# A hybrid scan and convolution layer on one core: the latent convolution's result kept in 8 KB rows and gathered by the loads, four scan output buffers, and one transfer per kernel block

## The chip, the cores and the metric

The kernel runs on one core of a Trainium2 chip. The metric is the device time of one execution in microseconds (us). The engines are TensorE (PE; PEld is its weight load), VectorE (DVE), ScalarE (ACT), GpSimd (POOL) and SyncE (SP). SPq and ACTq are the instruction queues of SP and ACT, from which transfers (DMAs) are issued in program order; sixteen DMA engines carry them.

## The reference

One layer of a diffusion backbone is computed for 256 context tokens and for 2048 latent tokens, which lie on a grid of 32 rows of 64. Each token's normalised and modulated vector is projected; one part goes through a bidirectional scan (SSD), another through a gated depthwise convolution, and both are joined in an output projection.

```python
h = rms_norm(x, g_pre) * (1 + scale) + shift
u = h @ w_in
z, xbc, dt_raw, ga, gb, gsil = jnp.split(u, [I_Z, I_XBC, I_DT, I_GA, I_GB], axis=-1)
y_ssd, h_fin = ssd_branch(z, xbc, dt_raw, ...)
# conformer_branch: convolution of 31 taps over the grid's rows, for each channel and column
h = ga * jax.nn.sigmoid(gb)
h = depthwise_conv(h, conv_w, conv_b)
h = layer_norm(h, ln_g, ln_b)
y_conf = jax.nn.silu(h) * jax.nn.silu(gsil)
out = jnp.concatenate([y_ssd, y_conf], axis=-1) @ w_out
return x + gate * rms_norm(out, g_post), h_fin
```

There are 1024 channels in the convolution, 1024 in the scan (16 heads of 64, state 128, chunks of 128 tokens). All is float32.

## The kernel before

The 2304 tokens are 18 tiles of 128: tiles 0 and 1 are context, 2 to 17 latent. Matmuls keep float32 accuracy by splitting each operand into a high and a low part and multiplying three pairs (`hh,wh`, `hl,wh`, `hh,wl`; lines L433 to L435).

The program has two halves (tiles 0 to 9, then 10 to 17). In each half `xbc_unit` projects the scan's inputs, `gab_unit` the convolution's (result `GL[j]`, by blocks `j` of 128 channels), `silu_unit` the gates. The weights' split parts are stored in the first half and loaded again in the second (`wh<-whd` L390, `wl<-wld` L391, three buffers each).

Beside the projections of the second half run two side streams. One is the scan, `pass_a(i)`, tile by tile: `xT` and `bc` are loaded (L705, L707), decay rows `lb` come by ACTq (L718), are masked on POOL (L730), exponentiated on ACT (L738) and combined on DVE (L742); `skip` (L810) begins the output `yg` of each of two groups, `close` (L815, L817) finishes it and stores it to `YP` (L818). The other is the latent convolution, `lat_conv(j)`: for 128 channels the grid rows `x` (`cx`, L671) and the banded kernel matrices `kd` (L670) are loaded one block ahead; ACT copies `kd` to `kt` (L679); PE does 256 small matmuls `cp` (L690); DVE adds the bias into `vt` (`cvv`, L694), in which a partition holds one of four groups of 32 channels and one grid row, with 32 channels x 64 columns behind it; four stores (L699) write it to `CV`, laid out as channels x tokens.

Then comes the out-projection, from tile 17 down. For each tile `conf_load` reads the 1024 channels of 128 tokens from `CV` (tile `cn`, two buffers, L1183), `conf_sum`, `conf_mean` and so on normalise it, and PE multiplies. The calls in the steady loop are written in program order and kept there for DVE, ACT and PE (those instructions carry the line L81 of the helper); elsewhere, and for the transfers, a list scheduler that works on estimated times sets each engine's order, within which an engine takes its instructions one after the other. A buffer with n copies can be written again only when the readers of the copy n uses before are done.

Of the kernel before, what the change touches and what calls it, by code (L numbers as in the profile page):

```python
# [8 lines left out]
F32 = mybir.dt.float32  # L9
# [8 lines left out]
P = 128  # L18
D = 1024
KT = D // P  # L20
NH = 16
HD = 64
NT = 18
NCTX = 2
# [60 lines left out]
def backbone_kernel(ctx, tc, xa, xt_in, cols, rows, wconv, conf_b, gp_row, bg_row, state0, w_mod, w_dt, w_in, w_out,  # L85
# [3 lines left out]
    V, S, T, DMA = (InOrder(tc, e) for e in (nc.vector, nc.scalar, nc.tensor, nc.sync))  # L89
# [5 lines left out]
    def bank(tag, name):  # L95
        return psp.tile([P, 512], F32, tag=tag, name=name, bufs=3 if tag == "mm" else 5)

    def dram(name, shape):
        return drp.tile(shape, F32, tag=name, name=name)
# [3 lines left out]
    ZS = [dram(f"zs{h}", [D, HT[h] * P]) for h in range(2)]  # L103
    GL = [dram(f"gl{j}", [P, NT * P]) for j in range(KT)]
    GS = [dram(f"gs{h}", [D, HT[h] * P]) for h in range(2)]
    CV = dram("cv", [D, NT * P])
    YP = [dram(f"yp{i}", [P, D]) for i in range(NT)]
    ST = [dram(f"st{i}", [P, D]) for i in range(NT)]
    LT = [dram(f"lt{h}", [HT[h] * 32, P]) for h in range(2)]
# [10 lines left out]
    def place(i):  # L120

        return (0, i) if i < HT[0] else (1, i - HT[0])
# [14 lines left out]
    cv = const.tile([P, NCOL], F32, name="cv")  # L137
# [51 lines left out]
    pa = ph_a.enter_context(tc.tile_pool(name="pa", bufs=1))  # L189
# [450 lines left out]
    def ctx_conv(j, tile):  # L640
        g = tile(f"cg{j}")
        G.memset(g[:, 0:15], 0.0)
        G.memset(g[:, 271:286], 0.0)
        DMA.dma_start(g[:, 15:271], GL[j][:, 0:256])
        yield
        acc = g[:, 512:768]
        w0 = C_CONFW + j * CW
        V.here("tensor_scalar", acc, g[:, 0:256], cv[:, w0:w0 + 1], cfb2[:, j:j + 1], MUL, ADD)
        for t in range(1, CW):
            V.here("scalar_tensor_tensor", acc, g[:, t:t + 256], cv[:, w0 + t:w0 + t + 1], acc, MUL, ADD)  # L650
            if t % 3 == 0:
                yield
        o = g[:, 768:1024]
        S.mul(o, acc, 0.5)
        DMA.dma_start(CV[j * P:(j + 1) * P, 0:256], o)
        yield


# [4 lines left out]
    def lat_load(j, lp):  # L663
        kd = lp.tile([P, 32, 32], F32, tag="kd", name=f"kd{j}", bufs=2)
        x = lp.tile([P, 32, 64], F32, tag="cx", name=f"cx{j}", bufs=2)
        lat_in[j] = kd, x
        for a in range(4):
            rs = slice(a * 32, (a + 1) * 32)
            src = bass.AP(tensor=wconv.tensor, offset=(j * 4 + a) * 64 * 32, ap=[[32, 32], [1, 1024]])
            DMA.dma_start(kd[rs].rearrange("p r g -> p (r g)"), src)  # L670
            DMA.dma_start(x[rs], GL[j][:, 256:].rearrange("(g a) (r w) -> a r g w", a=4, w=64)[a])  # L671

    def lat_conv(j, lp, cbb, more):
        if j not in lat_in:
            lat_load(j, lp)
        kd, x = lat_in.pop(j)
        yield
        kt = lp.tile([P, 32, 32], F32, tag="kt", name=f"kt{j}", bufs=1)
        S.copy(kt[:, :, ::-1].rearrange("p g r -> p r g"), kd)  # L679
        if more(j + 1):  # L680
            lat_load(j + 1, lp)
        yield
        vt = lp.tile([P, 32, 64], F32, tag="cvv", name=f"cvv{j}", bufs=1)
        for h in range(2):
            ps = {a: bank("ss", f"cp{j}_{a}") for a in (2 * h, 2 * h + 1)}
            for q in range(8):
                for u in range(4):
                    for a in ps:
                        rs = slice(a * 32, (a + 1) * 32)
                        T.matmul(ps[a][u * 32:(u + 1) * 32, q * 64:(q + 1) * 64], kt[rs, u * 8 + q, :], x[rs, u * 8 + q, :],  # L690
                                 start=True, stop=True)
            yield
            for a in ps:
                V.scalar_tensor_tensor(vt[:, a::4, :], ps[a].rearrange("p (c w) -> p c w", w=64), 0.5,  # L694
                                       cbb[:, j, a::4].unsqueeze(2).to_broadcast([P, 8, 64]), MUL, ADD)
            yield
        for u in range(4):
            c0 = j * P + u * 32
            DMA.dma_start(CV[c0:c0 + 32, 256:].rearrange("c (r w) -> r c w", w=64), vt[u * 32:(u + 1) * 32])  # L699


    def pass_a(i):
        half, il = place(i)
# [102 lines left out]
        yg = {}  # L806

        def skip(g):
            yg[g] = pa.tile([P, 4, P], F32, tag="yg", name=f"yg{i}{g}", bufs=2)
            V.tensor_tensor(yg[g], xT[:, 4 * g:4 * g + 4, :],  # L810
                            cv[:, C_D + 4 * g:C_D + 4 * g + 4].unsqueeze(2).to_broadcast([P, 4, P]), MUL)

# [35 lines left out]
        decay(0, 1)  # L848
        mask(1, 0)
        skip(0)  # L850
        load_lb(1, 1)
        yield
        weigh(0, 1)
        mix(0, 1)
        decay(1, 0)
        mask(1, 1)
        skip(1)
        yield
        diag(0, 0)
# [131 lines left out]
    V.tensor_tensor(wd4[:, :, 1, :], wdr, wd4[:, :, 0, :].bitcast(F32), SUB)  # L991
    xbc_phase(0, first, hb, [hprep(2, hb), hprep(0, hb)], tails, dt_post(0))
    extra = chain([gate_rows()] + [ctx_conv(j, big) for j in range(4)])
    interleave(post(0, 6), merge(scan(range(9)), 68, extra, 9 + 4 * 13), 90 * 8)
    last = [silu_unit(0, GS0, GS, j, hb, (2, 1, 0)) for j in (6, 7)]
# [19 lines left out]
    lp = ph_l.enter_context(tc.tile_pool(name="lp", bufs=1, side="right"))  # L1015
# [4 lines left out]
    blocks = post(1, 5)  # L1020
    cg = lambda name: lp.tile([P, D], F32, tag="cg", name=name, bufs=2)
    lat = lambda j: lat_conv(j, lp, cbb, gl_done.__contains__)
    extra = chain(f for j in range(4) for f in (lat(2 * j), ctx_conv(j + 4, cg), lat(2 * j + 1)))
    sc_ = scan(range(9, NT))
    run(take(blocks, 24))
# [112 lines left out]
    def norms(i, yz, nq):  # L1138

        pm = bank("ss", f"pm{i}")  # L1140
        src = [(c, e, t[1]) for c, e, t in ((0, 4.0 * EPS, yz), (1, EPS, nq)) if t]
        for c, e, t in src:
            T.matmul(pm[:, c:c + 1], t, ones[:, 0:1], start=True, stop=True)
        rs = []
        for c, e, t in src:
            ms = p1.tile([P, 1], F32, tag=f"ms{c}", name=f"yms{i}{c}", bufs=2)
            V.tensor_scalar(ms, pm[:, c:c + 1], 1.0 / D, e, MUL, ADD)
            rs.append((c, rstd_of(p1, ms, f"yr{i}{c}")))
        return rs
# [30 lines left out]

    def conf_load(i):
        n = p2.tile([P, 8, P], F32, tag="cn", name=f"cn{i}", bufs=2)
        DMA.dma_start(n, CV[:, i * P:(i + 1) * P].rearrange("(c p) t -> p c t", p=P))  # L1183
        return n

    def conf_sum(i, n):
        v = p2.tile([P, 8, P], F32, tag="v", name=f"v{i}", bufs=2)
        return v, sum8(v[:, 0, :], v[:, 0:4, :], n)
# [16 lines left out]
    def gs_load(i):  # L1205
        gs = p2.tile([P, 8, P], F32, tag="gs", name=f"gsl{i}", bufs=1)
        DMA.dma_start(gs, chan_slice(GS, i))
        return gs
# [57 lines left out]
    i = order[0]  # L1266
# [21 lines left out]
    for b in range(2):  # L1288
        for m, u in enumerate(last):
            run(take(u, 8))  # L1290
            if b == 0 and m == 1:
                rs = norms(i, yz, None)
# [3 lines left out]
            if b == 0 and m == 2:  # L1296
                ssd_scale(i, yz[0], spread(i, rs))
                yh = hl(p0, "y", 2, i, yz[0])
                lo(yh)
                yz = y_sum(i1)  # L1300
                for g in range(2):
                    state_decay(i1, g)
                ph_b[1].close()
                p2 = ph_1.enter_context(tc.tile_pool(name="p2", bufs=1))
                nn = [conf_load(i), conf_load(i1)]
                vv = [conf_sum(j, n) for j, n in zip((i, i1), nn)]
                for (v, t), j, n in zip(vv, (i, i1), nn):
                    conf_centre(n, conf_mean(j, t))
                    conf_square(v, n)
                nq = conf_sqsum(i, vv[0][0])  # L1310
            if b == 1 and m == 0:
                rs = norms(i, None, nq)
                nq = conf_sqsum(i1, vv[1][0])
            if b == 1 and m == 1:
                n, v = nn[0], vv[0][0]
# [3 lines left out]
            if b == 1 and m == 2:  # L1319
                gs0, v0, n = gs_load(i), v, nn[1]  # L1320
# [6 lines left out]
    for k in range(9, 13):  # L1327
        wo_load(k, wo4)
    n2 = conf_load(order[2])

    def out_seg(i, y, p, k0, k1):
# [6 lines left out]
    i, nxt, nx2 = order[:3]  # L1338
    banks(i)
    out_part(pso[i], yh, 0, 1)  # L1340
    rs = norms(nxt, yz, nq)
# [21 lines left out]
    v2, t = conf_sum(nx2, n2)  # L1363
# [18 lines left out]
    yz = y_sum(nx2)  # L1382
    ssd_load(order[3])
    n, n2 = n2, conf_load(order[3])
    yh = yhn

    for a, i in enumerate(order[1:], 1):
        last = a + 1 == NT
        e = {1: 4, 2: 2}.get(a, 0)
# [5 lines left out]
        rs = None if last else norms(nxt, yz, nq)  # L1395
# [6 lines left out]
        if nx2 is not None:  # L1402
            st_load(nx2)
            v2, t = conf_sum(nx2, n2)
# [37 lines left out]
        if a + 3 < NT:  # L1442
            ssd_load(order[a + 3])
            n, n2 = n2, conf_load(order[a + 3])
        else:
            n = n2
# [72 lines left out]
```

## Time and profile before

| what | value |
|---|---|
| median of three runs | 1862.05 us (1860.89 to 1865.44) |
| the profiled execution, its time / its span | 1862.69 / 1860.9 us |
| busy share of the span: PE, DVE, ACT, POOL | 97%, 65%, 47%, 9% |
| mean granted clock of PE | 0.983 |
| DMA packets, moved | 304253, 375.22 MB |
| of them under 512 B | 84198 |

The span is what lies between the first and the last instruction of the profile. In a row of the timeline the columns are start, duration, engine, line, operation, output and inputs, count, and in brackets the engine's idle time just before with what ended it. A line like L81 can be a helper's. "issue" means that the profile shows nothing that was waited for.

### The profile page before, as it was taken

What the parts mean: (1) busy time and instruction counts of PE and PEld (TensorE: products, weight loads), DVE (VectorE), ACT (ScalarE), POOL (GpSimd) and SP (SyncE); (2) the same over time, 40 slices, a digit from 0 to 9 for tenths busy, and PEclk for the clock granted to TensorE, in tenths of its full rate; (3) what the DMA queues carried; (4) which work ended last, traced back from release to release, by engine and by line L of the source; (5) the groups of instructions that cost most, each with busy time, mean ns of one, the idle gap of its engine ahead of it and who ended that gap; (6) DMA issues with size and microseconds to landing.
All of it is one profiled execution on the core that took longest, in us unless ns stands there. A gap on an engine that the chain in (4) does not pass through costs nothing.

```text
span 1860.9 us, 29891 instructions
## 1 busy us (share of the span) xinstructions
PE 1797.5 (97%) x11167; PEld 1482.9 (80%) x11167; DVE 1212.7 (65%) x1846; ACT 867.4 (47%) x1958; POOL 167.5 (9%) x281
## 2 busy tenths in 40 slices
PE   5899999999999999999999889899999999999998
PEld 3688887888888888888877667677887888888886
DVE  4488867565666762587457475868347887777763
ACT  4646424444465441834235445553245545454441
POOL 0002001111111000100001011110000111111110
PEclk9899999999999999999999899899999999999999
DMA  9556565574776664446598799685877666566632
GB/s 319 201 202 224 198 222 196 168 237 153 239 271 232 202 214 162 163 152 210 175 223 239 163 255 227 220 226 193 278 237 247 184 184 170 173 171 170 187 102 79
DMA packets 304253, 375.22 MB, mean 202 GB/s; under 512 B 84198, under 2 KB 203622, under 8 KB 304108
## 3 DMA queue, kind: packets, MB, share of 16 engines
q1 hardware_dynamic: 283372, 335.56, 58.1%
q10 hardware_dynamic: 20736, 37.76, 7.1%
q8 instruction: 88, 1.44, 0.3%
q14 instruction: 57, 0.47, 0.1%
HBM read 243.66 MB, written 129.59 MB: 201 GB/s over the span
## 4 chain that ended last, share of the span: by engine, by line
PE 84%; DMA 8%; ACT 2%; DVE 2%; issue 1%; SPq 1%; POOL 0%; ACTq 0%; POOLq 0%; DVEq 0%
PE op L81 20%; PE sp L433 7%; PE sp L434 7%; PE sp L435 7%; PE xp L434 5%; PE xp L435 5%; PE xp L433 5%; PE ga L433 3%; PE ga L435 2%; PE ga L434 2%; DMA lb<-lt 2%; PE gb L433 2%; PE gb L435 2%; PE gb L434 2%; PE py L774 2%; PE po L781 2%
## 5 line engine op out<-in xcount | busy, mean ns | idle before, releaser
L738 ACT ACTIVATE lb<-lb,WB 128x128 f32<-128x128 f32 x576 | 184.4, 391 | 173.5 <-POOL lb L730 159.6
L433 PE MATMUL sp<-hh,wh 128*128 128x512 f32 (+1 forms) x640 | 239.9, 375 | 0.0
L435 PE MATMUL sp<-hh,wl 128*128 128x512 f32 (+1 forms) x640 | 237.3, 371 | 0.0
L434 PE MATMUL sp<-hl,wh 128*128 128x512 f32 (+1 forms) x640 | 237.3, 371 | 0.0
L433 PE MATMUL xp<-hh,wh 128*128 128x512 f32 (+1 forms) x464 | 171.4, 371 | 2.0 <-ACT hh L329 2.0
L434 PE MATMUL xp<-hl,wh 128*128 128x512 f32 (+1 forms) x464 | 171.7, 370 | 0.0
L435 PE MATMUL xp<-hh,wl 128*128 128x512 f32 (+1 forms) x464 | 171.5, 370 | 0.0
L730 POOL TENSOR_SCALAR_AFFINE_SELECT lb<-lb 128x512 f32<-128x512 f32 x144 | 105.2, 733 | 730.4 <-ACT el L727 392.1
L530 DVE SCALAR_TENSOR_TENSOR cva<-raw,cwh,cva 128x1280 f32<-128x1280 f32 (+1 forms) x96 | 142.0, 1487 | 19.6 <-ACT cva L524 17.6
L435 PEld LDWEIGHTS sp<-hh,wl 128*128 128x128 f32 x640 | 121.4, 190 | 21.1
L433 PEld LDWEIGHTS sp<-hh,wh 128*128 128x128 f32 x640 | 121.7, 190 | 20.6
L434 PEld LDWEIGHTS sp<-hl,wh 128*128 128x128 f32 x640 | 121.6, 190 | 20.0
L433 PE MATMUL ga<-hh,wh 128*128 128x512 f32 (+1 forms) x320 | 121.1, 378 | 5.0 <-DMA wh<-whd 4.7
L75 DVE SCALAR_TENSOR_TENSOR cg<-cg,cv 128x256 f32<-128x256 f32 x240 | 121.2, 505 | 3.3
L433 PE MATMUL gb<-hh,wh 128*128 128x512 f32 (+1 forms) x320 | 120.4, 376 | 0.6 <-DVE gth L597 0.6
L435 PE MATMUL ga<-hh,wl 128*128 128x512 f32 (+1 forms) x320 | 119.1, 372 | 0.0
L434 PE MATMUL ga<-hl,wh 128*128 128x512 f32 (+1 forms) x320 | 118.8, 371 | 0.0
L435 PE MATMUL gb<-hh,wl 128*128 128x512 f32 (+1 forms) x320 | 118.5, 370 | 0.0
L434 PE MATMUL gb<-hl,wh 128*128 128x512 f32 (+1 forms) x320 | 118.4, 370 | 0.0
L742 DVE TENSOR_TENSOR lb<-lb,lb 128x512 f32<-128x512 f32 x72 | 50.5, 702 | 92.0 <-ACT lb L738 70.6
L433 PEld LDWEIGHTS xp<-hh,wh 128*128 128x128 f32 x464 | 88.1, 190 | 16.9 <-ACT hh L329 2.3
L434 PEld LDWEIGHTS xp<-hl,wh 128*128 128x128 f32 x464 | 87.9, 189 | 14.3
(269 smaller groups left out, 3758.6 us busy)
## 6 DMA issues: line engine op xcount, KB each, us to landing
lb<-lt ACTq DMA_DIRECT2D x144, 256.0 KB, 4.4
wr<-in_w_in SPq DMA_DIRECT2D x88, 256.0 KB, 5.4
whd<-wh SPq DMA_DIRECT2D x44, 512.0 KB, 4.0
wld<-wl SPq DMA_DIRECT2D x44, 512.0 KB, 5.2
wh<-whd SPq DMA_DIRECT2D x44, 512.0 KB, 4.3
wl<-wld SPq DMA_DIRECT2D x44, 512.0 KB, 5.9
xT<-xb SPq DMA_DIRECT2D x18, 512.0 KB, 4.1
yp<-yg SPq DMA_DIRECT2D x36, 256.0 KB, 4.6
```

Of the source, the lines that this page charges most:

```text
L75: return self._tc.keep_in_program_order(getattr(self._eng, name)(*a, **k))
L81: return lambda *a, **k: self._tc.keep_in_program_order(f(*a, **k))
L433: T.matmul(ps[:, :BN], wh[:, k, :], hh[:, k, :], start=(k == 0), stop=False)
L434: T.matmul(ps[:, :BN], wh[:, k, :], hl[:, k, :], start=False, stop=False)
L435: T.matmul(ps[:, :BN], wl[:, k, :], hh[:, k, :], start=False, stop=(k == KT - 1))
L530: V.scalar_tensor_tensor(a[:, :n], raw[:, t:t + n], cwh[:, ct * 5 + t:ct * 5 + t + 1], a[:, :n], MUL, ADD)
L730: G.affine_select(E[g, hq, d], E[g, hq, d], pattern=[[0, 4], [sg, P]], compare_op=ALU.is_ge, fill=NEG, base=0, channel_multiplier=-sg)
L738: S.activation(lb[:, h, :], lb[:, h, :], AF.Exp, bias=WB[:, i, c + h:c + h + 1])
L742: V.tensor_tensor(a, a, E[g, hq, 1], ADD)
L774: T.matmul(py[g][j * HD:(j + 1) * HD, q * P:(q + 1) * P], xt[g][:, h * HD:(h + 1) * HD], E[g, hq, 0][:, t, :], start=True, stop=True)
L781: T.matmul(po[g][:, q * P:(q + 1) * P], Sf[g][:, q * P:(q + 1) * P], bc[:, 2 + g, :], start=True, stop=True)
```

## The change

There are three edits. The latent part of the convolution's result gets a buffer of its own, `CVL`, whose row holds all channels of a block for one grid row: a partition of `vt` is stored as one run of 8 KB, and a tile of 128 tokens (two grid rows) is loaded by two transfers, each of 1024 runs of 256 B. The context's part goes to `CVC`. In the second half's tiles the `yg` buffers are four, in the pool `lp`. The kernel matrices of a block come in one transfer with a source of three dimensions.

```diff
-    CV = dram("cv", [D, NT * P])
+    CVC = dram("cvc", [D, NCTX * P])
+    CVL = dram("cvl", [KT * 32, P * 64])
...
-        DMA.dma_start(CV[j * P:(j + 1) * P, 0:256], o)
+        DMA.dma_start(CVC[j * P:(j + 1) * P, :], o)
...
+        src = bass.AP(tensor=wconv.tensor, offset=j * 4 * 64 * 32, ap=[[64 * 32, 4], [32, 32], [1, 1024]])
+        DMA.dma_start(kd.rearrange("p r g -> p (r g)"), src)
         for a in range(4):
             rs = slice(a * 32, (a + 1) * 32)
-            src = bass.AP(tensor=wconv.tensor, offset=(j * 4 + a) * 64 * 32, ap=[[32, 32], [1, 1024]])
-            DMA.dma_start(kd[rs].rearrange("p r g -> p (r g)"), src)
             DMA.dma_start(x[rs], GL[j][:, 256:].rearrange("(g a) (r w) -> a r g w", a=4, w=64)[a])
...
         for u in range(4):
-            c0 = j * P + u * 32
-            DMA.dma_start(CV[c0:c0 + 32, 256:].rearrange("c (r w) -> r c w", w=64), vt[u * 32:(u + 1) * 32])
+            DMA.dma_start(CVL[j * 32:(j + 1) * 32, u * 2048:(u + 1) * 2048],
+                          vt[u * 32:(u + 1) * 32].rearrange("r c w -> r (c w)"))
...
-            yg[g] = pa.tile([P, 4, P], F32, tag="yg", name=f"yg{i}{g}", bufs=2)
+            pool, n = (lp, 4) if half else (pa, 2)
+            yg[g] = pool.tile([P, 4, P], F32, tag="yg", name=f"yg{i}{g}", bufs=n)
...
-        DMA.dma_start(n, CV[:, i * P:(i + 1) * P].rearrange("(c p) t -> p c t", p=P))
+        if i < NCTX:
+            DMA.dma_start(n, CVC[:, i * P:(i + 1) * P].rearrange("(c p) t -> p c t", p=P))
+        else:
+            for e in range(2):
+                DMA.dma_start(n[:, :, e * 64:(e + 1) * 64],
+                              CVL.rearrange("(j r) (p w) -> r p j w", r=32, w=64)[2 * (i - NCTX) + e])
```

The scheduler orders the side streams anew. Three places follow; numbers at the end of a name count tiles and differ between the two programs, and so do line numbers (in the changed kernel L669 is the kernel load, L672 `cx`, L699 still the store, L812 `skip`, L817 and L819 `close`, L743 the sum of decay rows).

DVE, in the scan beside the projection of block 3 (`lb` decay rows, `yg` the scan's output, `gth` the convolution's gated input). Before:

```order
L742 TENSOR_TENSOR lb_9381<-lb_9381,lb_9383 128x512
L810 TENSOR_TENSOR yg_9621<-xT_9249,cv 128x512
L597 SCALAR_TENSOR_TENSOR gth_3_3_9258<-gth_3_3_9258,ga_3_3_9260 128x512
L815 TENSOR_TENSOR yg_9147<-yg_9147,py_9284 128x512
L817 TENSOR_TENSOR yg_9147<-yg_9147,yo_9360 128x512
```

After:

```order
L743 TENSOR_TENSOR lb_9373<-lb_9373,lb_9375 128x512
L598 SCALAR_TENSOR_TENSOR gth_3_3_9256<-gth_3_3_9256,ga_3_3_9258 128x512
L743 TENSOR_TENSOR lb_9491<-lb_9491,lb_9493 128x512
L817 TENSOR_TENSOR yg_9145<-yg_9145,py_9282 128x512
L819 TENSOR_TENSOR yg_9145<-yg_9145,yo_9352 128x512
```

The next tile's `skip` no longer stands between two decay sums ahead of this tile's `close`; it has been moved further up, and a decay sum takes its place.

SP, at the stores of the third convolution block (`kd` kernels, `cv` or `cvl` the stored result, `bc` scan inputs, `wh` and `wl` weights). Before:

```order
L670 DMA kd_10786<-in_wconv 32x1024
L699 DMA cv<-cvv_9751 32x32x64 x4
L707 DMA bc_10303<-xb_64 128x4x128
L670 DMA kd_10786<-in_wconv 32x1024 x3
L390 DMA wh_1_9637<-whd_137 128x1024
L391 DMA wl_1_9636<-wld_181 128x1024
```

After:

```order
L669 DMA kd_10772<-in_wconv 128x1x1024
L699 DMA cvl<-cvv_9740 32x2048 x4
L708 DMA bc_10292<-xb_64 128x4x128
L391 DMA wh_1_9629<-whd_138 128x1024
L392 DMA wl_1_9628<-wld_182 128x1024
```

Three kernel transfers between the stores and the weights are gone.

SP, ahead of the first convolution block (`gl` the stored gated input, `cx` the grid rows read from it, `cg` context input). Before:

```order
L598 DMA gl_68<-gth_0_4_8389 128x512
L670 DMA kd_9314<-in_wconv 32x1024 x2
L670 DMA kd_9335<-in_wconv 32x1024 x4
L644 DMA cg_9984<-gl_73 128x256
L671 DMA cx_8588<-gl_68 32x32x64 x4
```

After:

```order
L391 DMA wh_1_8430<-whd_143 128x1024
L392 DMA wl_1_8429<-wld_187 128x1024
L599 DMA gl_68<-gth_0_4_8390 128x512
L669 DMA kd_9330<-in_wconv 128x1x1024
L672 DMA cx_8589<-gl_68 32x32x64 x4
```

The third block's kernels still stand between the store and the loads that read it, now as one transfer; two more kernel transfers and the context load have moved ahead of the weights.

In the out-projection the order is as before, with two `cn` loads at each place where one stood.

## The prediction

> **What bounds the kernel.** I read the page first, then the busy time by stage, then the idle gaps of TensorE (PE) and what ended each, and last the queue of SyncE (SPq), which issues almost every transfer.
>
> ```profile
> PE   5899999999999999999999889899999999999998
> PEclk9899999999999999999999899899999999999999
> ```
>
> Each digit is a fortieth of the span. PE is full except at the start, at the end and in slices 21 to 26; there its granted clock falls too. The table by stage says how much is lost (columns: window, PE busy, PEld, DVE, ACT, POOL, granted clock, share of the 16 DMA engines, GB/s):
>
> ```profile
> 120.00:900.00 780.00, 779.07 (x4185) 654.05 (x4184) 524.70 (x753) 372.33 (x810) 69.95 (x128) 1.00 0.60 202
> 900.00:1260.00 360.00, 334.24 (x3342) 266.08 (x3341) 222.20 (x375) 163.90 (x396) 40.33 (x64) 0.95 0.84 218
> 1260.00:1440.00 180.00, 177.65 (x1111) 145.45 (x1110) 110.03 (x163) 73.12 (x147) 5.58 (x8) 1.00 0.74 239
> 1440.00:1800.00 360.00, 360.00 (x1769) 303.40 (x1768) 274.80 (x416) 181.51 (x464) 40.23 (x45) 1.00 0.61 170
> ```
>
> From 120 to 900 us and from 1440 to 1800 us PE has no idle time to give back. From 900 to 1260 us, where the latent convolution and the scan of tiles 10 to 17 run beside the projections, it idles 360 - 334.2 = 25.8 us and loses about 334.2 x 0.05 = 16.7 us to a lower clock: 42.5 us at most. All three edits act there, and the first also acts in the out-projection.
>
> The three largest gaps of PE there, with the DVE waits behind two of them (idle time and releaser in brackets):
>
> ```profile
> 1012.96 2.03 PE L690 MATMUL cp<-cx,kt 32*32 32x64 f32 x122 [4.56 <-DVE yg L815]
> 1062.29 0.79 PE L787 MATMUL pst<-xwh,bth 128*128 128x512 f32 x1 [5.13 <-DVE cvv L694]
> 1080.86 0.77 PE L433 MATMUL ga<-hh,wh 128*128 128x512 f32 x1 [4.68 <-DMA wh<-whd]
> ...
> 1011.01 0.69 DVE L810 TENSOR_TENSOR yg<-xT,cv 128x512 f32<-128x512 f32 x1 [4.44 <-DMA yp<-yg]
> 1060.34 0.69 DVE L810 TENSOR_TENSOR yg<-xT,cv 128x512 f32<-128x512 f32 x1 [8.95 <-DMA yp<-yg]
> ```
>
> At 1011 and 1060 us DVE stands still until a `yg` buffer has been stored; the sum L815 and the `cvv` result, on which PE waits, come behind that in its order. The third gap is a weight tile that came late. Why the stores and weights are late stands in SPq's own order:
>
> ```profile
> 1048.46 6.21 SPq L671 DMA_DIRECT2D cx<-gl  x4
> 1054.76 1.27 SPq L818 DMA_DIRECT2D yp<-yg  x1
> ...
> 1064.52 4.72 SPq L699 DMA_DIRECT2D cv<-cvv  x4
> ...
> 1070.65 2.52 SPq L670 DMA_DIRECT2D kd<-in_wconv  x3
> 1073.27 0.37 SPq L390 DMA_DIRECT2D wh<-whd  x1
> ```
>
> The `yp` store that freed DVE was issued behind 6.2 us of `cx` loads; the weight that PE lacked was issued behind 4.7 us of `cv` stores and 2.5 us of `kd` loads, and PE started 7.6 us after its issue.
>
> **Four scan buffers (L810).** Each tile uses two `yg` buffers, so with four a tile needs those of two tiles before, whose stores have long landed; DVE's two waits go. PE's gaps go with them: 4.56 + 5.13 = 9.7 us. After each gap PE ran at a lower clock:
>
> ```profile
> 1010.00:1020.00 10.00, 7.04 (x139) 5.90 (x140) 5.66 (x9) 7.51 (x22) 2.87 (x6) 0.66 0.55 169
> 1060.00:1070.00 10.00, 7.71 (x33) 6.64 (x34) 7.31 (x13) 5.91 (x12) 1.27 (x2) 0.70 0.67 151
> 1080.00:1090.00 10.00, 9.14 (x35) 6.69 (x36) 7.97 (x16) 3.45 (x10) 1.59 (x2) 0.67 0.88 306
> ...
> 1190.00:1200.00 10.00, 7.00 (x21) 5.55 (x21) 6.78 (x12) 6.94 (x20) 2.69 (x4) 0.54 0.45 156
> ```
>
> 7.04 x 0.34 = 2.4 us and 7.71 x 0.30 = 2.3 us. Together 14.4 us. What is late next is DVE's wait for ScalarE's decay row, which stood behind the first of them:
>
> ```profile
> 1015.76 0.69 DVE L742 TENSOR_TENSOR lb<-lb,lb 128x512 f32<-128x512 f32 x1 [2.13 <-ACT lb L738]
> ```
>
> PE was not idle there, so I charge nothing for it and keep it as a rival. The buffers cost no instruction; the same L810 run at other places of DVE's order and wait only for `xT`.
>
> **Stores of 8 KB (L699) and kernels in one transfer (L670).** Counts stay 32 for the stores; kernels go from 32 transfers to 8.
>
> ```profile
> L699 SPq DMA_DIRECT2D cv<-cvv x32: 318/994/3030, 958.1 to 1309.1; - x32
> L670 SPq DMA_DIRECT2D kd<-in_wconv x32: 311/420/1633, 920.7 to 1167.7; - x32
> ...
> L390 SPq DMA_DIRECT2D wh<-whd x44: 319/320/3022, 733.7 to 1373.3; - x44
> ...
> DMA packets 100630, 78.42 MB, mean 218 GB/s; under 512 B 66766, under 2 KB 80462, under 8 KB 100593
> ```
>
> The three issue rows give minimum, median and maximum in ns. Of the 66,766 packets under 512 B in the window, 28 stores x 1024 pieces of 256 B = 28,672 go. A store in long rows should issue like a weight load, 0.32 us in place of 0.99: 32 x 0.67 = 21 us of SPq, and 24 kernel issues x 0.42 = 10 us. SPq is not the bound; what counts is who was queued behind, and that is the third gap, 4.68 us, with 9.14 x 0.33 = 3.0 us of clock: 7.7 us. The weight moves up by 4.7 - 4 x 0.32 + 2 x 0.42 = 4.3 us of issue (of the three kernel issues ahead of it one stays), and earlier still as `cvv` itself is no longer late. But PE also arrives 5.1 us earlier, since the gap before it goes. Bounds 0 and -7.7; the shift is of the gap's size while the consumer moves as much, so I take the middle, -3.9 us.
>
> The context's own buffer changes 8 stores of 128 KB in row pitch alone, beside full PE: nothing.
>
> **Loads that gather (L1183).** Each of 16 latent tiles is loaded by two transfers of 1024 pieces of 256 B in place of one with pieces of 512 B. The nearest row is `cx`, also 256 KB in 256 B pieces (landing in us: minimum, median, maximum, first `cx`, then `cn`):
>
> ```profile
> L671 SPq DMA_DIRECT2D cx<-gl x32: 318/1037/3301, 937.5 to 1226.2; - x32
> ...
> DMA to landing us min/median/max: 4.3/6.3/10.4
> ...
> L1183 SPq DMA_DIRECT2D cn<-cv x18: 360/371/568, 1391.9 to 1772.2; - x18
> ...
> DMA to landing us min/median/max: 4.0/5.0/7.4
> ```
>
> Where such a load has time, and where not:
>
> ```profile
> 1573.55 0.37 SPq L1183 DMA_DIRECT2D cn<-cv  x1
> ...
> 1590.50 0.68 DVE L81 TENSOR_TENSOR v<-cn 128x512 f32<-128x512 f32 x1
> ...
> 1395.88 0.69 DVE L1068 TENSOR_TENSOR v<-cn 128x512 f32<-128x512 f32 x1 [1.71 <-DMA cn<-cv]
> ...
> 1410.18 0.49 PE L1154 MATMUL pn<-ident,yr 128*128 128x128 f32 x2 [0.88 <-POOL yr L152]
> ```
>
> In the steady out-projection the load is issued 17.0 us before DVE's first sum reads it. Even `cx`'s slowest landing with a second issue ahead, 10.4 + 1.0 = 11.4 us, fits: nothing on the path. Queued behind it are the decay rows and the gate, each a few tenths of a us later, with PE at 360.0 of 360 us. If that cover went, each tile would pay what exceeds 17 us. At the start of the phase DVE waits for the first load and PE, 14 us on, for the norm that follows. Two tiles land (6.3 - 5.0) x 2 = 2.6 us later; bounds 0 and 2 x (10.4 - 5.0) = 10.8; I take +2.6, for the `cx` median was taken under a fuller DMA (0.84 against 0.74).
>
> **Sum.** -14.4 - 3.9 + 2.6 = -15.7 us. The profiled execution took 1862.7 us (span 1860.9), 0.6 above the median of 1862.05; on the median that is 1846 us. About 0.3%, 5.6 us, is what a measurement of this kernel can tell from no change.
>
> **Rivals.**
> Four engines for the kernels: the new `kd` source has an outermost count of 4 where each old transfer had 32 rows. If a transfer is dealt out by that count, four engines move 128 KB each.
>
> ```profile
> 1340.00:1350.00 10.00, 10.00 (x45) 8.27 (x45) 2.75 (x3) 3.49 (x4) 0.00 (x0) 1.00 1.07 383
> ...
> 944.03 1.46 PE L690 MATMUL cp<-cx,kt 32*32 32x64 f32 x126 [0.29 <-DMA cx<-gl]
> ```
>
> At a full DMA 16 engines moved 383 GB/s, 24 each: 128 KB take 5.5 us against 1.4 us over sixteen. The first `cx` loads stand right behind the third kernel transfer and PE already waits for them at 944 us: 4.1 us of gap and some 2.4 us of clock (as at 1010 us), and the weight behind a kernel gains nothing. -14.4 + 6.5 + 2.6 = -5.3: 1857 us. For it: the shape; against: every later kernel transfer stands well ahead of the loads that go with it. Chance 0.2. The Trainium skill (DMA: Bandwidth & Descriptors, section "Why a DMA increments its semaphore by 16 and not by 1") speaks for it: the number of engines is the largest up to 16 that divides the slowest non-1 count on both sides. By that rule it is four here, and the rival's 1857 us would be the forecast; no row of this trace has such a transfer.
>
> The waits move: freed of `yg`, DVE meets late decay rows, weights still come late, and PE's gaps only shift. With all of the -14.4 and -3.9 refilled but for a few us, some 1861 us. For it: DVE's L742 waits; against: PE did not idle on those. Chance 0.15.
>
> Slower, by bunching: SPq, no longer held, issues weight pairs back to back ahead of ScalarE's `lb` rows. Before shows one such place:
>
> ```profile
> 1174.70 0.88 ACTq L718 DMA_DIRECT2D lb<-lt  x2
> ...
> 1185.12 0.42 ACT L727 ACTIVATE el<-lb 64x256 f32<-64x256 f32 x1 [2.42 <-DMA lb<-lt]
> ...
> 1187.53 0.50 PE L787 MATMUL pst<-xwh,bth 128*128 128x512 f32 x1 [2.04 <-ACT xwh L764]
> ...
> 1193.18 1.09 PE L750 MATMUL px<-ident,xT 128*128 128x128 f32 x4 [3.00 <-issue]
> ```
>
> Rows issued at 1174.7 us were waited for until 1185.1; PE lost 2.04 + 3.00 and 7.00 x 0.46 = 3.2 us of clock: 8.2 us. Two new places cancel the gain, three end at 1846 + 24.6 = 1871 us. Against: the DMA carries less. Chance 0.1.
>
> More: the smaller gaps ease too. 42.5 - 22.1 = 20.4 us are left in the window; half of it gives 1836 us. Chance 0.1.
>
> **Chances.** The forecast, 1846 (1840 to 1853), 0.45; the rivals 0.2, 0.15, 0.1, 0.1. Range 1834 to 1861: it leaves out the slower case and the tails. Faster by over 0.3% (under 1856.5): 0.45 + 0.1 + about 0.16 of the four-engine and moved-wait cases = 0.71; within: 0.19; slower: 0.10.
>
> **What would show it.** DVE no longer waits for `yp<-yg` after 1000 us; L699 issues at about 0.32 us; packets under 512 B in the window fall by some 28,700; no gap of PE is ended by `wh`. PE's idle time from 900 to 1260 us should be about 11 us. Against me: a gap of 4 us or more before the first `cp`, kernel transfers that land later than the 6.3 us of `cx`, a gap at the first norm over 4 us, or clocks below 0.8 at new places.

## The result

| | before | after |
|---|---|---|
| median of the runs | 1861.47 us (1860.67 to 1865.44) | 1891.85 us (1887.47 to 1894.48) |
| ratio, 95% interval | | 1.0156 [1.0137, 1.0174] |
| span of the profiled execution, mean granted clock | 1860.9 us, 0.983 | 1889.7 us, 0.979 |

The changed kernel is 30 us slower where the prediction had 16 us faster. First the strip of the page of after: 40 equal slices of 47 us, busy share of PE and granted clock in tenths.

```profile
PE   5899999999999999999988887999999999999998
PEclk9899999999999999999988899999999999999999
```

The loss is where all three edits act. The table by stage of after (window, PE busy, PEld, DVE, ACT, POOL, clock, DMA share, GB/s):

```profile
900.00:1260.00 360.00, 315.14 (x3120) 249.29 (x3119) 206.64 (x346) 150.13 (x363) 38.30 (x59) 0.92 0.76 206
1260.00:1440.00 180.00, 174.33 (x1201) 141.94 (x1201) 103.81 (x163) 67.66 (x144) 7.36 (x11) 0.98 0.68 218
1440.00:1800.00 360.00, 358.06 (x1757) 300.90 (x1756) 276.85 (x411) 189.13 (x472) 39.08 (x44) 1.00 0.69 183
```

From 900 to 1260 us PE idles 360 - 315.1 = 44.9 us (before 25.8) and loses 315.1 x 0.08 = 25.2 us to the clock (before 16.7): 28 us more in this stage alone, and DMA is less busy than before (0.76 against 0.84). In the out-projection, where the gathering loads are, PE is busy for 358 of 360 us. PE's waits of after from 900 to 1320 us (who waits, for whom, us in total, times, longest):

```profile
PE cp L691 <- DMA cx<-gl: 11.8, 2, 10.9
PE px L751 <- DVE cvv L695: 8.6, 2, 8.1
PE cp L691 <- DVE yg L817: 7.3, 2, 6.6
PE cp L691 <- DVE cvv L695: 6.7, 1, 6.7
...
PE ga L434 <- DMA wh<-whd: 3.8, 1, 3.8
```

The 0.3 us that PE waited for the first `cx` has become 10.9 us, and there are three gaps on DVE of 6.6 to 8.1 us in place of two of 4.6 and 5.1. DVE no longer waits for the `yg` stores here; it waits for the decay rows longer than before:

```profile
DVE lb L743 <- ACT lb L739: 42.7, 10, 6.8
DVE btl L839 <- ACT bth L838: 24.0, 6, 11.4
DVE yg L812 <- issue: 16.3, 1, 16.3
```

These are DVE's waits of after from 900 to 1260 us; in the same stretch of before the first was 19.6 us. The third is one wait, which ends at 959.8 us; nothing in the records shows what ended it, but the load of `xT` that L812 reads was issued at 952.4 us, behind 8.8 us of `cx` loads. Where PE's 10.9 us come from stands in SPq's timeline of after:

```profile
919.93 0.66 SPq L669 DMA_DIRECT2D kd<-in_wconv  x1
...
921.69 0.58 SPq L669 DMA_DIRECT2D kd<-in_wconv  x1
...
928.45 0.38 SPq L599 DMA_DIRECT2D gl<-gth  x1
935.68 0.55 SPq L669 DMA_DIRECT2D kd<-in_wconv  x1
943.47 8.83 SPq L672 DMA_DIRECT2D cx<-gl  x4
```

and in the chain of waits of after:

```profile
928.45 15.01 DMA gl<-gth
943.47 0.33 SPq L672
943.85 10.62 DMA cx<-gl
```

The kernels cost little to issue. But the store of `gl`, issued behind two of them, lands after 15.0 us, and `cx`, issued behind a third, after 10.6 us (6.0 in before's chain; 15.0 and 10.6 us are times from issue to what waited). Transfers that have nothing to do with the kernels suffer too. The transfers from 930 to 1320 us, first of before, then of after (issues, KB each, median us from issue to landing; the kernels of after have no landing in the records):

```profile
yp<-yg SPq DMA_DIRECT2D x18, 256.0 KB, 5.0
...
kd<-in_wconv SPq DMA_DIRECT2D x26, 128.0 KB, 6.3
```

```profile
yp<-yg SPq DMA_DIRECT2D x16, 256.0 KB, 13.1
...
kd<-in_wconv SPq DMA_DIRECT2D x6, 512.0 KB
```

### The profile page after: what moved, and what is told of

It is laid out like the page before. It is cut to its first block, busy times and chain, and to the rows that moved or that the text cites. A ratio compares the mean times of both kernels' runs of the same rounds, so it can differ in the third digit from the quotient of the medians.

```text
span 1889.7 us, 29884 instructions
## 1 busy us (share of the span) xinstructions
PE 1801.2 (95%) x11167; PEld 1485.3 (79%) x11167; DVE 1214.4 (64%) x1846; ACT 869.2 (46%) x1958; POOL 168.4 (9%) x281
## 4 chain that ended last, share of the span: by engine, by line
PE 82%; DMA 10%; DVE 2%; ACT 2%; issue 2%; POOL 1%; SPq 0%; POOLq 0%; ACTq 0%; DVEq 0%
PE op L81 20%; PE sp L434 7%; PE sp L435 7%; PE sp L436 7%; PE xp L436 5%; PE xp L435 5%; DMA lb<-lt 5%; PE xp L434 5%; PE ga L434 2%; PE ga L436 2%; PE ga L435 2%; PE gb L434 2%; PE gb L435 2%; PE gb L436 2%; PE py L775 2%
## 5 line engine op out<-in xcount | busy, mean ns | idle before, releaser
L531 DVE SCALAR_TENSOR_TENSOR cva<-raw,cwh,cva 128x1280 f32<-128x1280 f32 (+1 forms) x96 | 141.8, 1485 | 20.8 <-ACT cva L525 18.7
L743 DVE TENSOR_TENSOR lb<-lb,lb 128x512 f32<-128x512 f32 x72 | 50.4, 700 | 113.7 <-ACT lb L739 93.0
L728 ACT ACTIVATE el<-lb 64x256 f32<-64x256 f32 x136 | 56.4, 415 | 96.5 <-DMA lb<-lt 74.8
```

What stands on the lines that cost most here:

```text
L531: V.scalar_tensor_tensor(a[:, :n], raw[:, t:t + n], cwh[:, ct * 5 + t:ct * 5 + t + 1], a[:, :n], MUL, ADD)
L728: S.activation(el[g][rs, q:q + 2, :], E[g, hq, 0][rs, j::2, :], AF.Exp)
L743: V.tensor_tensor(a, a, E[g, hq, 1], ADD)
```

## The experiments

Three theories stood at the start. F (few engines): the one kernel transfer, whose source has an outermost count of 4, is carried by four of the sixteen DMA engines, and all else that needs these engines queues behind it. L: the 8 KB rows with the gathering loads cost it. O: the other order of DVE and ACT, which four `yg` buffers bring, costs it. The table is read as a set of switches; the ratio is to the kernel before on the same chip.

| run | kernels `kd` | `yg` | stored rows | `lb` loads | median us | ratio [95%] |
|---|---|---|---|---|---|---|
| after | one transfer, 4 x 32 rows | 4 | 8 KB | as before | 1891.9 | 1.0156 [1.0137, 1.0174] |
| e1 | four of 32 rows | 4 | 8 KB | as before | 1872.0 | 1.0043 [1.0023, 1.0063] |
| e3 | one of 128 rows | 4 | 8 KB | as before | 1869.7 | 1.0031 [1.0009, 1.0053] |
| e6 | two of 2 x 32 rows | 4 | 8 KB | as before | 1935.9 | 1.0393 [1.0354, 1.0432] |
| e2 | one, 4 x 32 rows | 2 | 256 B | as before | 1890.3 | 1.0147 [1.0125, 1.0168] |
| e4 | four of 32 rows | 4 | 256 B | as before | 1861.7 | 0.9986 [0.9970, 1.0003] |
| e5 | four of 32 rows | 2 | 8 KB | as before | 1864.0 | 1.0011 [0.9993, 1.0028] |
| e7 | one of 128 rows | 2 | 256 B | as before | 1852.6 | 0.9950 [0.9929, 0.9972] |
| e8 | one of 128 rows | 4 | 256 B | as before | 1851.9 | 0.9952 [0.9934, 0.9969] |
| e10 | one of 128 rows | 2 | 8 KB | as before | 1859.9 | 0.9992 [0.9978, 1.0006] |
| e11 | one of 128 rows | 4 | 8 KB | earlier | 1858.5 | 0.9994 [0.9982, 1.0006] |
| e9 | one of 128 rows | 4 | 256 B | earlier | 1841.5 | 0.9908 [0.9876, 0.9940] |
| e12 | one of 128 rows | 2 | 256 B | earlier | 1852.5 | 0.9956 [0.9938, 0.9974] |
| e15 | one of 128 rows | 4 | 4 KB | earlier | 1857.7 | 0.9968 [0.9953, 0.9983] |
| e16 | one of 128 rows | 4 | 2 KB | earlier | 1868.5 | 1.0033 [1.0012, 1.0054] |
| e13 | one of 128 rows | 4 | 256 B, 264 B apart | earlier | 1900.8 | 1.0191 [1.0165, 1.0218] |
| e14 | one of 128 rows | 4 | 256 B, 264 B apart | as before | 1900.6 | 1.0196 [1.0168, 1.0225] |
| e17 | one of 128 rows | 4 | 256 B, 512 B apart | earlier | 1845.3 | 0.9916 [0.9884, 0.9948] |
| e18 | one of 128 rows | 4 | 256 B, 320 B apart | earlier | 1848.7 | 0.9922 [0.9899, 0.9945] |

"256 B" with no more said is the layout of before, channels x tokens, loaded by one transfer for each tile; all others are rows by grid row, loaded by the two gathering transfers.

**The kernel transfer.** e1 splits it again; e3 keeps one transfer and lays the matrices out beforehand as 128 rows of 4 KB; e6 makes two transfers whose outermost count is 2. e2 puts the transfer of after alone into before.

```diff
 # after
-        src = bass.AP(..., ap=[[64 * 32, 4], [32, 32], [1, 1024]])
-        DMA.dma_start(kd.rearrange("p r g -> p (r g)"), src)
 # e3
+        DMA.dma_start(kd.rearrange("p r g -> p (r g)"), wconv[j * P:(j + 1) * P, :])
 # e6
+        for e in range(2):
+            src = bass.AP(..., ap=[[64 * 32, 2], [32, 32], [1, 1024]])
+            DMA.dma_start(kd[e * 64:(e + 1) * 64].rearrange("p r g -> p (r g)"), src)
```

> The changed kernel with the kernel matrices in four transfers of 32 rows again. Theory F: 1842 to 1856 us, a few us more than with one transfer of 128 rows because of 24 more issues. Theory L and theory O: about 1890 us.

> The kernel before with the third edit alone: one kernel transfer whose source has the outermost count 4. Theory F: slower than before by 20 to 45 us (it lacks the four yg buffers and keeps the short stores), with a gap of about 10 us before the first small matmuls. Theories L and O: 1862 us or a little less, since 24 issues go.

> The changed kernel with one edit: the host lays the kernel matrices out as 8 x 128 rows of 4 KB, so the one transfer has 128 rows on both sides and no outermost count of 4. Orders of PE and SP are those of the changed kernel. Theory F (few engines: a transfer whose outermost count is 4 is carried by four of the sixteen engines, and what is queued behind it waits): the first grid rows land in time, no gap over 3 us before the first small matmuls, idle time of PE from 900 to 1260 us falls from 45 to about 12 us, time 1840 to 1852 us. Theory L (the 8 KB rows and the gathering loads cost it): no change, about 1890 us. Theory O (the new order of DVE and ACT, brought by the four yg buffers, costs it): no change, about 1890 us.

> The changed kernel with each block's kernel matrices in two transfers of 64 rows, whose source has the outermost count 2. Theory F: the count deals the transfer out, so now two engines carry 256 KB each per block (four carried 128 KB each), and it is slower than the changed kernel's 1892 us, by 20 to 60 us. A rival that blames the size of a transfer, or its three dimensions, or the scheduler's order, would have it between the one transfer (1892) and the four (1872): about 1880 us.

e2 alone gives 27 us (0.0147 x 1861), nearly the whole loss; e1 and e3 take 21 to 23 us of it away again ((1.0156 - 1.0043) x 1861 = 21, (1.0156 - 1.0031) x 1861 = 23). Neither e1 nor e3 came down to the 1856 and 1852 us that F alone foretold at most; what is left is the subject further down. Size and count of the transfers are the same in e3 and after. By the traces so are the orders of PE, POOL and SP, and those of DVE and ACT but for two and four places; what differs is the source, its shape and where it lies. That the place is not it shows e1, which reads the old addresses with 32 rows outermost. Singly, the three edits (e2, e4, e5) come to 0.0147 - 0.0014 + 0.0011 = 0.0144; together, in after, they measure 0.0156. SPq's timeline of e3, to be read against that of after:

```profile
925.63 0.43 SPq L668 DMA_DIRECT2D kd<-in_wconv  x1
...
927.49 0.45 SPq L668 DMA_DIRECT2D kd<-in_wconv  x1
...
931.27 0.32 SPq L599 DMA_DIRECT2D gl<-gth  x1
934.71 0.33 SPq L668 DMA_DIRECT2D kd<-in_wconv  x1
938.64 3.15 SPq L671 DMA_DIRECT2D cx<-gl  x4
```

From the `gl` store to the first `cx` load that waits for it are 7.4 us in place of 15.0, behind the same two transfers, and a kernel transfer lands in 6.7 us, `yp` in 6.4 instead of 13.1 us (transfers of e3 from 930 to 1320 us):

```profile
yp<-yg SPq DMA_DIRECT2D x17, 256.0 KB, 6.4
...
kd<-in_wconv SPq DMA_DIRECT2D x6, 512.0 KB, 6.7
```

e6 goes the other way: with a count of 2 the waits of PE from 900 to 1320 us, the stage of 900 to 1260 us and the chain are those of after, doubled:

```profile
PE cp L692 <- DMA cx<-gl: 22.6, 2, 21.8
PE cp L692 <- DVE cvv L696: 12.8, 1, 12.8
PE ga L434 <- ACT lb L740: 12.2, 1, 12.2
PE px L752 <- DVE cvv L696: 11.5, 1, 11.5
```

```profile
900.00:1260.00 360.00, 278.72 (x2556) 219.35 (x2555) 179.37 (x300) 126.76 (x304) 31.55 (x51) 0.89 0.65 178
```

Counts of 2, 4 and 128 give 1936, 1892 and 1870 us (with a count of 2 in two transfers of half the size), and the DMA share from 900 to 1260 us goes with them: 0.65, 0.76, 0.79. F holds. Which engines carried what is not in the records, so "few engines" is shown by this dose and by who waited, not engine by engine. The Trainium skill (DMA: Bandwidth & Descriptors, section "Why a DMA increments its semaphore by 16 and not by 1") states that the count of engines is the largest up to 16 that divides the slowest count above 1 on both sides: 2, 4 and 16 here. The three times agree with it in their order.

**Each other edit alone.**

```diff
 # e4: before, and only
+            pool, n = (lp, 4) if half else (pa, 2)
+            yg[g] = pool.tile([P, 4, P], F32, tag="yg", name=f"yg{i}{g}", bufs=n)
 # e5: after, with four kernel transfers and
+            yg[g] = pa.tile([P, 4, P], F32, tag="yg", name=f"yg{i}{g}", bufs=2)
```

> The kernel before with the second edit alone: four yg buffers in the second half. The prediction's step: 14.4 us less, 1848 us, with no DVE wait on stored yg after 1000 us. Theory O: slower than before by up to 28 us.

> The kernel before with the first edit alone: 8 KB rows, gathering loads, the context in a buffer of its own. Four yg buffers alone gave 1862 us and with the 8 KB rows 1872. If the rows cost that by themselves (theory L, in small), 1868 to 1876 us; if the two only collide (both move the waits to the decay rows), 1858 to 1866. The prediction had this edit at about 1860.

> The kernel before with the kernel matrices laid out by the host as 128 rows of 4 KB and loaded in one transfer per block. Theory F: no loss as with the outermost count of 4 (1890 us); 24 issues fewer, 1855 to 1864 us.

> The kernel before with four yg buffers and one kernel transfer of 128 rows, without the 8 KB rows. If both are worth a little each and the 8 KB rows cost what is left, 1852 to 1861 us, the fastest so far; if the waits only move on to the decay rows, 1860 to 1868 us.

The 8 KB rows alone do nothing that can be measured, and four `yg` alone give 2.6 us (0.0014 x 1861; the interval takes in no change), where the prediction had 14.4. DVE's waits of e4 from 900 to 1260 us:

```profile
DVE lb L742 <- ACT lb L738: 37.5, 11, 7.9
...
DVE yg L811 <- issue: 8.5, 1, 8.5
DVE yg L811 <- DMA xT<-xb: 6.5, 2, 6.2
```

The wait for `yp` (17.7 us in before) is gone and the one for decay rows is 18 us longer, with 6.5 us for `xT`. These are waits of DVE, though, and PE did gain in this stage: its idle time from 900 to 1260 us fell from 25.8 to 18.7 us and its clock rose from 0.95 to 0.97. From 1260 to 1320 us e4 loses some of it again: PE idles 3.4 us there at a clock of 0.97, where before has no idle time and 1.00. One kernel transfer of 128 rows alone is worth 9 us (e7), faster than the 1855 us expected at best, and four `yg` add nothing to it (e8).

**What is left in e3.** Against before its three edits come to 1.0031, though e4 and e5 are at zero and e7 is at -9 us. e8 against e3 shows 15 us ((1.0031 - 0.9952) x 1861) for the 8 KB rows, where e5 had none. L was open again, with two additions: that the rows hurt only with four `yg`, or that late decay rows are the cause. e10 is e3 with two `yg`; e9, e11 and e12 are e8, e3 and e7 with each call of `load_lb` one scan step earlier.

```diff
+        load_lb(0, 0)
         yield
-        load_lb(0, 0)
+        load_lb(0, 1)
         yield
 ...
         mask(0, 0)
-        load_lb(0, 1)
+        load_lb(1, 0)
```

> Before with the 8 KB rows and one kernel transfer of 128 rows of 4 KB, but two yg buffers; this is e3 without the four yg. Pairing (the loss of about 18 us between e8, 1852 us, and e3, 1870 us, needs four yg and the 8 KB rows together): 1850 to 1858 us, and ACT's wait for decay rows lb as short as in e7. Rows (the 8 KB rows cost it as soon as the kernels come in one transfer, yg is no part of it): 1866 to 1874 us, with DVE's wait for lb as long as in e3, about 44 us.

> e3 with each call of load_lb made one scan step earlier; no other edit. Late decay rows (ScalarE's rows lb, issued late on ACTq, are what e3's 18 us over e8 consist of): DVE's wait for lb falls from 44 us to below 25 us, and the time to 1850 to 1858 us. Elsewhere (the wait on lb is only the place where lateness shows; the loss comes from the order of DVE or from stores): 1866 to 1874 us, the wait moving to xT or yp.

> e8 (before with four yg and kernels of 128 rows) with each call of load_lb made one scan step earlier. Late decay rows: the 28.7 us of DVE's wait for lb in e8 halve, PE's idle time from 900 to 1260 us falls by 4 to 8 us, 1842 to 1848 us. Elsewhere: 1850 to 1854 us, as e8.

> Before with kernels of 128 rows (e7, 1852.6 us) and each call of load_lb made one scan step earlier, two yg buffers. Late decay rows: DVE's wait for lb was only 13.8 us in e7, and its wait for yp is left, so little: 1848 to 1854 us. Elsewhere: 1851 to 1856 us; slower than e9 only if four yg are worth something once lb is early.

e10 fits neither expectation: it lies at 1859.9 us, 8 us above e7 (0.0042 x 1861). So the rows cost some 8 us beside a good kernel transfer with two `yg` and 15 with four. Earlier decay rows take 7 us off e3 and 8 off e8, but DVE's wait for them in e9 did not halve as I expected, nor did it fall below 25 us in e11; that for `xT` fell in e9. DVE's waits from 900 to 1320 us, of e8 and then of e9:

```profile
DVE lb L741 <- ACT lb L737: 28.7, 10, 5.9
...
DVE yg L810 <- DMA xT<-xb: 13.9, 4, 7.4
```

```profile
DVE lb L741 <- ACT lb L737: 28.8, 10, 5.7
...
DVE yg L810 <- DMA xT<-xb: 2.6, 2, 1.4
```

So what the earlier call mends is not the lateness of `lb` that I had blamed. The timelines of e8 and then of e9 (DVE, PE) and the stage from 1260 to 1320 us show what it is:

```profile
1245.62 1.29 DVE L810 TENSOR_TENSOR yg<-xT,cv 128x512 f32<-128x512 f32 x2 [7.43 <-DMA xT<-xb]
1264.29 1.09 PE L749 MATMUL px<-ident,xT 128*128 128x128 f32 x4 [4.17 <-issue]
1260.00:1320.00 60.00, 55.83 (x507) 44.72 (x506) 39.02 (x65) 19.61 (x38) 1.34 (x2) 0.94 0.66 200
```

```profile
1239.46 1.29 DVE L810 TENSOR_TENSOR yg<-xT,cv 128x512 f32<-128x512 f32 x2
1255.90 0.63 PE L749 MATMUL px<-ident,xT 128*128 128x128 f32 x4 [1.53 <-issue]
1260.00:1320.00 60.00, 60.00 (x535) 48.32 (x535) 34.60 (x55) 18.18 (x31) 0.72 (x1) 1.00 0.77 237
```

In e8 the scheduler has moved the last tile's `skip` up so far that DVE stands 7.4 us for its `xT`; in e9 four other instructions stand ahead of it, the load is issued 5.6 us earlier (1231.4 against 1237.0 us), and it need not wait. From 900 to 1260 us the two kernels are alike (PE busy for 344.3 and 344.7 us, clock 0.99); from 1260 to 1320 us e8 loses 4.2 us of idle time and 55.8 x 0.06 = 3.3 us of clock, and e9 nothing. Together that is 7.5 us, about what e9 gains. The kernels with four `yg` and the old place of the call (after, e1, e3, e4 and e8) all have this wait (4.0 to 7.4 us) and, 18.7 us behind it, a gap of PE of 3.4 to 4.3 us at `px`. Those with two `yg` (before, e5, e7) or with the earlier call (e9, e11, e17) have no such wait, and no gap at `px` above 2.1 us after 1200 us. In e2 a wait of 7.1 us at L810 for `yp` is followed by the same gap, 3.9 us, again 18.7 us on; e16 has a wait of 4.4 us without the gap. What released `px` is not in the records, so the step from the wait to the gap is not shown and rests on this pattern.

Without four `yg` the earlier call does nothing (e12 against e7), with them 8 us: beside the kernel transfer of 128 rows term A's buffers are worth about 9 us (e9 against e12) once `skip` no longer waits. e11 is 16 us above e9 ((0.9994 - 0.9908) x 1861): the rows cost as much as before, and with them DVE still waits long for `lb` (DVE's waits of e11 from 900 to 1320 us):

```profile
DVE lb L742 <- ACT lb L738: 42.5, 11, 7.3
```

**Loads, long rows or order.** The scheduler gives other orders when the stores change: compared place by place in the traces, 181 of DVE's 1846 instructions and 112 of ACT's 1958 differ between e9 and e11. e13 puts the channels of a row 66 numbers apart instead of 64, so that a store is again 1024 pieces of 256 B while the two gathering loads stay, at the new pitch; ACT's order is then that of e9, DVE's up to 6 rows. e14 is the same on e3, e17 has 128 and e18 80 numbers; e13, e17 and e18 have the same order on every engine. e15 and e16 are e11 with each store cut in two of 4 KB rows and four of 2 KB rows.

```diff
-    CVL = dram("cvl", [KT * 32, P * 64])
+    CVL = dram("cvl", [KT * 32, P * 66])
-            DMA.dma_start(CVL[j * 32:(j + 1) * 32, u * 2048:(u + 1) * 2048], ...)
+            DMA.dma_start(CVL[j * 32:(j + 1) * 32].rearrange("r (p w) -> r p w", w=66)[:, u * 32:(u + 1) * 32, :64],
+                          vt[u * 32:(u + 1) * 32])
```

> e11 (8 KB rows with gather, four yg, kernels of 128 rows, earlier decay rows; 1858.5 us) with the 128 channels of a row 66 instead of 64 numbers apart, so that a store writes 1024 pieces of 256 B as before; the gathering loads stay. The scheduler then orders ACT as in e9 and DVE up to 6 rows as in e9 (1841.5 us). Stores or order (the 17 us belong to the long-row stores or to the order of DVE and ACT that the scheduler makes for them): 1840 to 1847 us. Loads (the two gathering loads of each tile cost it): 1854 to 1860 us.

> The same edit on e3 (1870 us), with the decay rows at their old place; ACT in the order of e8, DVE up to 6 rows (1852 us). Stores or order: 1849 to 1856 us. Loads: 1866 to 1872 us.

> e11 with each store of 8 KB rows cut in two of 4 KB rows; the scheduler's order differs from that of e11 in 44 rows of DVE and 74 of ACT, none of PE. Stores (long pieces themselves cost): 1854 to 1862 us, as e11. Order (the 17 us are the luck of one order): could be anywhere from 1841 to 1865 us; more than 5 us away from e11 speaks for it.

> e11 with each store cut in four of 32 rows of 2 KB; 153 rows of DVE and 207 of ACT differ from e11, more from e9. Stores: between e9 and e11 but near e11, 1850 to 1862 us. Order: anywhere from 1841 to 1865 us; e15 and e16 both within 3 us of e11, with orders that differ, would speak against it.

> e13 with the channels of a row 128 instead of 66 numbers apart; every engine's order is that of e13, stores are pieces of 256 B, now 512 B apart. Stores or order (the long-row stores or the order made for them cost e11 its 17 us, and e13's loss came from its odd pitch of 264 B alone): 1840 to 1847 us, store landing back from 14.6 to about 5.5 us. Loads (the two gathering loads per tile cost it): 1854 to 1860 us. Order of e13 (e13's loss was not the pitch): about 1900 us, landing over 10 us.

> The same with 80 numbers, 320 B, between the channels of a row; the same order again. If pieces that begin at a multiple of 64 B are enough, as e17; if the pieces must begin at a multiple of more than 64 B, the store's landing stays over 10 us and the time is near e13's, 1895 to 1905 us.

(e16's label is wrong; its pieces are 2 KB, as the text on it says.) e16 lies above both its expectations (1865 us at most). e13 and e14 missed all theirs by 29 us or more, and told of something else: the landing of the stores. The same row of the transfers from 900 to 1320 us, of e13, of e18 and of e17:

```profile
cvl<-cvv SPq DMA_DIRECT2D x28, 256.0 KB, 14.6
```

```profile
cvl<-cvv SPq DMA_DIRECT2D x32, 256.0 KB, 6.4
```

```profile
cvl<-cvv SPq DMA_DIRECT2D x32, 256.0 KB, 5.6
```

Pieces that begin 264 B apart land in 14.6 us, 320 B apart in 6.4, 512 B apart in 5.6, in one and the same order of all engines; the times are 1900.8, 1848.7 and 1845.3 us. With that cost out of the way e17 answers the question: it has the gathering loads and the time of e9 (0.9916 against 0.9908, 1.5 us apart, each known to about 6 us), 14 us below e11. **It is not the gathering loads that cost e11 its time; it is the long-row stores, or the order that the scheduler makes for them.** DVE's wait for `lb` in e17 from 900 to 1320 us is again the short one:

```profile
DVE lb L742 <- ACT lb L738: 24.6, 9, 6.3
```

Between these two the runs don't decide. For the order: e15 and e16 hold pieces of 4 and 2 KB under other orders and lie 5 us below and 7 us above e11 by their ratios, and an 8 KB row lands no later than short pieces (5.3 us in e11, 5.5 in e9). Nor do the decay rows: they land in 4.7 us in e11, 5.3 in e9 and 5.4 in e17 (medians from 930 to 1320 us), though ACT waits for them 50.6, 23.6 and 18.4 us (from 900 to 1320 us). So in e11 they are asked for late, not carried slowly. How much of the 16 us that is worth is not shown: in e5 ACT waits 42.7 us for them, at no cost that can be measured, and in e16, the slowest of e9, e11, e15 and e16, DVE waits only 23.0 us for `lb`. Against: every kernel with pieces of 2 KB or more beside four `yg` and the good kernel transfer lies at 0.9968 or above, and every one with short pieces at the other pitches at 0.9952 or below. Long rows under the order of short ones were not tried; this stays open.

## Why the prediction was wrong

- **The four-engine rival was the right mechanism, priced at a quarter.** The forecast's own sum put the new shape of the `kd` source at nothing, and the rival that priced it put it at 6.5 us; e2 measures 27. The step that failed is this price, with the sentence "every later kernel transfer stands well ahead of the loads that go with it". I took the 4.1 us that one transfer holds four engines longer, put it once ahead of the first `cx`, and asked afterwards only whether the kernels themselves come in time. They do; but whatever is issued behind them and needs the same engines waits. Measured: two transfers ahead of `gl`, 7.6 us more from its issue to the loads that need it (15.0 - 7.4, after against e3); one ahead of `cx`, 4.6 us more (10.6 - 6.0, after against before). So 4.1 us for each transfer was about right, and counting one of eight was not: `yp` lands 6.7 us later in the median (13.1 - 6.4, after against e3). In all 23 to 27 us (after against e3, e2 against before). The shape was in the diff and the rule was known; I gave it 0.2 because no row of the trace of before showed such a transfer, and let the low price keep it within the range.
- **Term A, -14.4 us, measured -2.6.** The wait and its gaps were right: with four `yg` DVE's wait for `yp` is gone, and from 900 to 1260 us PE has 7.0 us less idle time in e4 (25.8 - 18.7) and some 6 us less loss by the clock (0.97 in place of 0.95), in one execution each. The step that failed is "the same L810 run at other places of DVE's order and wait only for `xT`", with that wait put at nothing. The last tile's L810 waits 6.2 us for `xT` in e4, and PE loses 3.4 us of idle time and 1.7 of clock from 1260 to 1320 us. This is the second rival, the waits move, but the wait that counts is the one for `xT` and not, as I had it, the one for `lb`. e9 against e12 shows 9 us for the same buffers where L810 does not wait. What else e4 lost of the stage's gain was not found; its profiled execution is 4.2 us below that of before.
- **Term B, -3.9 us.** Two assumptions failed: that a store in long rows issues like a weight load, and that the weight would then come in time.

```profile
L699 SPq DMA_DIRECT2D cvl<-cvv x32: 303/556/1870, 969.3 to 1336.4; - x32
```

  That is the row of after (minimum, median, maximum in ns): the minimum is near the 0.32 us that I took, the median 0.56; four of them took 2.4 to 4.2 us on SPq in e3. The wait for the weight stayed at 3.8 us in after. What the kernels in one transfer can bring is e7's 9 us, with 128 rows. The packets under 512 B fell as forecast, from 70,080 to 36,668 between 930 and 1320 us, and brought nothing (e5): DMA's packet count was not what bound this stage.
- **Term C, +2.6 us, was not seen.** At the start of the out-projection DVE waits 1.9 us for `cn` in after and 1.7 in before, and PE 0.9 us for the first norm in both. Between e17 and e9 a cost of 2.6 us would not show.
- Of the signs named beforehand, DVE's freedom from `yp` after 1000 us and the packets came true. PE's idle time from 900 to 1260 us did not, with 44.9 us in place of 11. Two of the signs against me came true as well: a gap over 4 us ahead of the first `cp`, and right behind it a clock of 0.56. The row of after (columns as in the table by stage):

```profile
950.00:960.00 10.00, 5.87 (x139) 4.82 (x140) 0.17 (x1) 0.00 (x0) 0.00 (x0) 0.56 0.94 215
```

  Of the third rival, weights bunched ahead of the `lb` rows, little was seen: ACT's wait for these rows did grow from 29.1 to 46.3 us from 900 to 1320 us, but it is 48.1 us in e3 too, where they land in 4.7 us in the median as against 4.9 in before.

## What to carry to other kernels

Look at the outermost counts of both sides of a transfer before merging several into one: one transfer with 128 rows outermost was 9 us better than four of 32 rows (2 us beside the other two edits, e3 against e1), the same bytes with 4 outermost were 27 us worse, and the cost fell on other transfers behind it in the queue. Price a buffer by the wait that its user meets next at its new place in the order: four `yg` gave nothing that could be measured while `skip` stood waiting for `xT`, alone or beside the good kernel transfer, and 9 us where it did not. The fastest kernel of this study is e9, 0.9908 [0.9876, 0.9940] of before: kernels of 128 rows, four `yg`, earlier decay rows, and the stores as they were.

## What was not expected of the hardware

A store of 1024 pieces of 256 B took 14.6 us to land where the pieces began 264 B apart in memory, 6.4 us at 320 B and 5.6 us at 512 B (medians from 900 to 1320 us), with the same order on every engine; the kernel lost 52 to 56 us to the pitch of 264 B (1900.8 against 1848.7 and 1845.3; 50 to 51 by the ratios). The gathering loads, which read the same rows in pieces of 256 B, did not suffer: a `cn` load landed in 4.4, 4.2 and 4.8 us. No run shows why, or which pitches are bad. A transfer whose source has an outermost count of 4 slowed transfers of other tensors that were issued behind it, `yp` from 6.4 us (e3) to 13.1 (after), while the DMA engines' mean busy share from 900 to 1260 us fell from 0.79 to 0.76.
